# Opening of a decoder trunk: the first tiles of x on two DMA queues, the positions behind them

## The chip, the cores and the metric

The kernel runs on one core of a Trainium2 chip. The metric is the device time of one execution in microseconds (us). Five engines of the core work side by side, each through its own instructions in order: TensorE (PE in the rows, its weight loads PEld), VectorE (DVE), ScalarE (ACT), GpSimd (POOL) and SyncE (SP), which only issues DMAs here. A DMA that SP or ACT issues is put into that engine's queue; all queues share 16 DMA engines. An instruction that waits holds up everything behind it on its engine.

## The reference, cut to what matters

Two layers of a conditioned decoder trunk on x, 512 tokens of width 1024, in float32. Each layer normalises x, modulates it by a vector made from the condition c, and multiplies by a wide weight matrix. Cut to what the opening of the kernel computes:

```python
cos, sin = rope_tables(positions, x.dtype)
c_act = jax.nn.silu(c)
ada = jnp.einsum('bd,de->be', c_act, w_ada[l]) + b_ada[l]
sh_m, sc_m, g_m, sh_f, sc_f, g_f = jnp.split(ada, N_ADA, axis=-1)
h = modulate(rmsnorm(x, norm_mix_g[l]), sh_m, sc_m)
proj = jnp.einsum('bsd,de->bse', h, w_in[l])
# ... convolutions, differential attention, gates, MLP, a second layer, final norm
```

## The kernel before, in words

Activations lie transposed on the chip: 128 features on the partitions, 512 tokens along the row. So x, which comes in eight tiles `xin[2 * i + hh]` of 128 tokens and 512 features (256 KB each, tile family `cv`), is turned on TensorE by 128x128 transposes into eight tiles `xT[0]` to `xT[7]`. The four tiles of hh = 0 hold what `xT[0]` to `xT[3]` need, the four of hh = 1 the rest. Each turn (`x_turned`) is four transposes into one of three PSUM buffers of the family `t`, and one copy out of it by ACT (a unit `x`) or by DVE (a unit `v`).

The order of the opening is written out by hand in the string `START`. A unit is a letter and a number: `x`, `v` turn x; `y` squares a tile of x on ACT for the norm; `i` steps the task that loads and turns the parameter rows (`prm`); `a` steps `angles`, the rotary angles on DVE from the positions; `e`, `d` are the parts of the first modulation vectors that DVE sums up (into `part`), `r`, `s` the parts that TensorE sums up from `w_ada`; `c`, `t`, `q` bring these to columns (`ada`, `gsc`); `n`, `b` make the norm's factor and spread it; `m` makes a pair of h tiles from xT; `h`, `l` split a quarter of a weight tile into a rounded part and its remainder; `p` is a share of the first four products. Each engine sees its own instructions of these units in this order.

`w_ada` and the first weights of `w_in` come in four quarters, each of eight and two DMAs of 256 KB, all on SP behind x (families `qk`, `o`, `v`, `raw`). The DMAs of SP and ACT take turns on eight semaphores; an issue waits until the DMA that had its semaphore before has landed, so up to eight are under way. In the opening before, SP issues the positions (256 KB, the same 2 KB row to 128 partitions), then the eight tiles of x; ACT issues c and the small table `rc`; POOL the parameter rows. After the opening a planner keeps TensorE fed, and nothing there has a fixed time.

The second pair of h tiles (unit `m1`) stands on DVE behind unit `e2`, which reads the last `o` tile of the third quarter; TensorE's product `p6` reads that pair.

Of the kernel before, what the change touches and what calls it, by code (L numbers as in the profile page):

```python
# [17 lines left out]
P = 128  # L18
D = 1024
S = 512  # L20
# [14 lines left out]

ON_DVE = ((2, 3), (1, 5), (8, 3), (3, 7))
START = (
# [39 lines left out]
def kernel(  # L77
# [7 lines left out]
    nc = tc.nc  # L85
    V, A, T, G = nc.vector, nc.scalar, nc.tensor, nc.gpsimd
# [19 lines left out]
    def slot(tag, dt=F32, shape=None):  # L106
        return slots.tile(shape or [P, S], dt, tag=tag, name=nm(tag), bufs=SLOTS[tag])
# [79 lines left out]
    def params(l, eng=None):  # L187

        prm[l] = const.tile([P, NROW], F32, name=f"prm{l}")
        groups = (  # L190
            (
                (C_BADA, 48, b_ada[l].rearrange("(a p) -> a p", p=P)),
                (C_NMIX, 8, norm_mix_g[l].rearrange("(a p) -> a p", p=P)),
            ),
            (
                (C_NMLP, 8, norm_mlp_g[l].rearrange("(a p) -> a p", p=P)),
                (C_CAB, 4, conv_a_b[l].rearrange("(a p) -> a p", p=P)),
                (C_LNG, 4, ln_a_g[l].rearrange("(a p) -> a p", p=P)),
                (C_LNB, 4, ln_a_b[l].rearrange("(a p) -> a p", p=P)),
                (C_CBW, 12, conv_b_w[l].rearrange("k (a p) -> (k a) p", p=P)),  # L200
                (C_SUB, 1, subln_g[l].rearrange("(a p) -> a p", p=P)),
                (C_FG, 8, final_g.rearrange("(a p) -> a p", p=P)),
            ),
        )
        for gi, grp in enumerate(groups):
            c0, n = grp[0][0], sum(g[1] for g in grp)
            prow = ftile(F32, [n, P])
            for r0, m_, src in grp:
                G.dma_start(prow[r0 - c0 : r0 - c0 + m_, :], src)
            yield 15  # L210
            pt = ps_t()
            T.transpose(pt[:, :n], prow, ident[:n, :n])
            yield 1
            V.tensor_copy(prm[l][:, c0 : c0 + n], pt[:, :n])
            written.add((l, gi))
            yield 1
        V.tensor_scalar(out=subg[:, l : l + 1], in0=prm[l][:, C_SUB : C_SUB + 1],
                        scalar1=1.0 - lam_init[l], scalar2=None, op0=ALU.mult)
        written.add((l, "sub"))
# [900 lines left out]
    crow = ftile(F32, [8, P])  # L1120
    A.dma_start(crow, c.rearrange("b (a p) -> (b a) p", p=P))
    rc = const.tile([P, 2], F32, name="rc")
    A.dma_start(rc, rope_c)
    posi = slot("at", I32)
    nc.sync.dma_start(posi, positions.to_broadcast([P, S]))
    prm_task = params(0)
    next(prm_task)
    x2 = x.rearrange("b s d -> (b s) d")
    xin = [None] * 8
    for hh in range(2):  # L1130
        for i in range(NTB):
            t = xin[2 * i + hh] = slot("cv")
            nc.sync.dma_start(t, x2[i * P : (i + 1) * P, hh * 512 : (hh + 1) * 512])
    stage = iter(["qk"] * 16 + ["o"] * 8 + ["v"] * 8)

    def fetch(v, qt):
# [85 lines left out]
    def turn(row):  # L1222

        pt = ps_t()
        for a in range(4):
            T.transpose(pt[:, a * P : a * P + P], row[:, a * P : a * P + P], ident)
        return pt
# [92 lines left out]
    def rows_copy(qt):  # L1320
# [8 lines left out]
        i=lambda _: next(prm_task),  # L1329
        z=lambda _: next(lam_task),  # L1330
# [8 lines left out]
        t=lambda qt: q_cols.update({qt: turn(q_rows[qt])}),  # L1339
# [61 lines left out]
```

## Time and profile before

| what | value |
|---|---|
| time, median of 3 runs | 1890.07 us (1889.49 to 1890.42) |
| the profiled execution's own time | 1890.15 us |
| its span, first to last instruction | 1888.4 us |
| PE busy | 1868.8 us, 99% of the span |
| DVE, ACT, POOL busy | 66%, 42%, 3% |
| chain that ended last, by engine | PE 96%, DMA 2%, DVE 1% |

The span is followed from its first instruction; the profiled execution is 1.75 us longer than it. The chain of work that ended last is followed back from the last instruction, at each step to what released it. Idle time of an engine is printed with what ended it. A PE row that reads busy may still hold short waits, since ends of matmuls are modelled.

### The profile page before, as it was taken

How to read it: one execution, taken by the hardware profiler on the slowest of the kernel's cores; microseconds unless marked ns; L12 is line 12 of the kernel's file. 1: busy time of each engine (PE TensorE's matmuls, PEld its weight loads, DVE VectorE, ACT ScalarE, POOL GpSimd, SP SyncE). 2: the span in 40 equal slices, each digit the busy share in tenths (PEclk: the TensorE clock that was granted, in tenths of full speed). 3: DMA queues.
4: the chain of work that ended last, by engine and by line, in shares of the span. 5: the costliest groups of instructions: out<-in, count | busy, mean ns of one | idle time of the engine just before them, and what ended most of it. 6: DMA issues, size and time to landing. Idle time of an engine off the chain costs nothing.

```text
span 1888.4 us, 24857 instructions
## 1 busy us (share of the span) xinstructions
PE 1868.8 (99%) x9565; PEld 1597.4 (85%) x9565; DVE 1254.1 (66%) x2139; ACT 788.5 (42%) x1428; POOL 62.8 (3%) x109
## 2 busy tenths in 40 slices
PE   8999999999999999999999999999999999999998
PEld 6888888888889888888898888888888898888888
DVE  7788678997776656565677887798764563333336
ACT  4666652222433524233445665322243353424253
POOL 2001010000000000000000000000000000000000
PEclk9999999999999999999999999999999999999999
DMA  8644323444454455555535442222223422232221
GB/s 274 180 131 125 94 90 106 128 135 158 149 195 128 150 183 182 178 187 186 168 99 145 127 123 90 82 97 89 90 79 100 142 82 89 90 105 96 90 90 68
DMA packets 211142, 240.67 MB, mean 127 GB/s; under 512 B 10280, under 2 KB 178352, under 8 KB 211024
## 3 DMA queue, kind: packets, MB, share of 16 engines
q1 hardware_dynamic: 210096, 238.85, 40.5%
q8 instruction: 75, 1.23, 0.3%
q0 software_dynamic: 768, 0.23, 0.1%
q14 instruction: 43, 0.35, 0.1%
q10 hardware_dynamic: 160, 0.01, 0.0%
HBM read 216.50 MB, written 2.10 MB: 116 GB/s over the span
## 4 chain that ended last, share of the span: by engine, by line
PE 96%; DMA 2%; DVE 1%; issue 0%; SPq 0%; ACT 0%; POOLq 0%; POOL 0%; DVEq 0%; ACTq 0%
PE mm L150 86%; PE s L150 3%; PE t L827 2%; PE s L798 1%; PE s L797 1%; PE t L815 1%; DMA qk<-in_w_ada_dram 1%; PE t L460 0%; PE t L308 0%; PE t L835 0%; DMA f<-f 0%; DMA o<-in_w_ada_dram 0%; DMA cv<-in_x_dram 0%; DMA raw<-in_w_in_dram 0%; PE t L452 0%
## 5 line engine op out<-in xcount | busy, mean ns | idle before, releaser
L150 PE MATMUL mm<-h,wh 128*128 128x512 f32 x2720 | 850.7, 392 | 0.0
L150 PEld LDWEIGHTS mm<-h,wh 128*128 128x128 f32 x2720 | 508.0, 188 | 102.5 <-issue 0.7
L150 PE MATMUL mm<-h,wl 128*128 128x512 f32 x1360 | 532.1, 391 | 0.0
L399 ACT CAST wh<-raw 128x1024 fp32r<-128x1024 f32 (+1 forms) x308 | 308.7, 1005 | 404.2 <-PE mm L150 354.7
L407 DVE TENSOR_TENSOR wl<-raw,wh 128x1024 fp32r<-128x1024 f32 (+1 forms) x308 | 357.9, 1166 | 78.5 <-ACT wh L399 75.6
L150 PE MATMUL mm<-qk,wh 128*128 128x512 f32 (+1 forms) x1024 | 300.5, 376 | 0.0
L150 PEld LDWEIGHTS mm<-h,wl 128*128 128x128 f32 x1360 | 255.5, 188 | 52.1 <-issue 0.2
L150 PEld LDWEIGHTS mm<-qk,wh 128*128 128x128 f32 x1024 | 188.2, 188 | 35.1
L150 PE MATMUL mm<-qk,wl 128*128 128x512 f32 (+1 forms) x512 | 192.6, 376 | 0.0
L935 DVE SCALAR_TENSOR_TENSOR cv<-v,caw,cv 128x511 f32<-128x511 f32 (+14 forms) x240 | 175.9, 733 | 4.0
L504 DVE SCALAR_TENSOR_TENSOR xT<-mm,ada,xT 128x512 f32<-128x512 f32 (+1 forms) x81 | 56.0, 691 | 151.6 <-PE mm L150 151.5
L286 DVE SCALAR_TENSOR_TENSOR araw<-araw,cact,araw 128x512 f32<-128x512 f32 x140 | 104.6, 747 | 23.1 <-DMA araw<-in_w_ada_dram 22.7
L150 PEld LDWEIGHTS mm<-qk,wl 128*128 128x128 f32 x512 | 96.4, 188 | 17.2
L1082 ACT ACTIVATE f<-mm 128x512 f32<-128x512 f32 x60 | 35.9, 598 | 160.6 <-PE mm L150 157.1
L150 PE MATMUL mm<-o,wh 128*128 128x512 f32 (+1 forms) x320 | 95.2, 380 | 0.0
L150 PE MATMUL mm<-v,wh 128*128 128x512 f32 (+1 forms) x320 | 94.9, 379 | 0.0
L150 PE MATMUL mm<-wh,h 128*128 128x256 f32 x448 | 85.1, 284 | 0.0
L768 ACT ACTIVATE cv<-cv,st 128x128 f32<-128x128 f32 (+3 forms) x128 | 70.9, 556 | 18.3 <-DVE st L761 17.9
L1049 ACT ACTIVATE f<-mm 128x512 f32<-128x512 f32 x38 | 22.7, 598 | 132.4 <-PE mm L150 132.3
L443 POOL TENSOR_TENSOR st<-st,nhalf 128x4 f32<-128x4 f32 (+2 forms) x29 | 32.2, 1111 | 1360.9 <-DVE st L465 1007.5
L1056 DVE SCALAR_TENSOR_TENSOR f<-f,mm 128x512 f32<-128x512 f32 x38 | 26.1, 687 | 76.2 <-PE mm L150 76.1
L474 DVE TENSOR_TENSOR qk<-f,qk 128x512 fp32r<-128x512 f32 x38 | 26.3, 691 | 74.3 <-ACT qk L471 74.2
(263 smaller groups left out, 2324.8 us busy)
## 6 DMA issues: line engine op xcount, KB each, us to landing
raw<-in_w_in_dram SPq DMA_DIRECT2D x66, 1024.0 KB, 5.2
raw<-in_w_ff_dram SPq DMA_DIRECT2D x64, 1024.0 KB, 5.3
araw<-in_w_ada_dram SPq DMA_DIRECT2D x160, 256.0 KB, 2.9
raw<-in_w_c_out_dram SPq DMA_DIRECT2D x8, 1024.0 KB, 5.0
raw<-in_w_out_dram SPq DMA_DIRECT2D x8, 1024.0 KB, 5.1
f<-f SPq DMA_DIRECT2D x120, 64.0 KB, 2.1
qk<-qk SPq DMA_DIRECT2D x48, 128.0 KB, 2.3
qk<-in_w_ada_dram SPq DMA_DIRECT2D x16, 256.0 KB, 6.0
```

What stands on the lines that cost most here:

```text
L150: T.matmul(ps, lhsT, rhs, start=start, stop=stop)
L286: V.scalar_tensor_tensor(out=part, in0=r, scalar=cact[:, k : k + 1], in1=part, op0=ALU.mult, op1=ALU.add)
L399: A.copy(h_, r_)
L407: V.tensor_tensor(l_, r_, h_.bitcast(F32), op=ALU.subtract)
L443: G.tensor_tensor(y, v[:, :n], nhalf[:, :n], op=ALU.pow)
L474: V.tensor_tensor(lo, src, hi.bitcast(F32), op=ALU.subtract)
L504: V.scalar_tensor_tensor(out=xT[e][:, t0:t1], in0=pp[:, t0:t1], scalar=g[:, e : e + 1], in1=xT[e][:, t0:t1], op0=ALU.mult, op1=ALU.add)
L768: A.activation(p[cc][:, :n], p[cc][:, :n], AF.Exp, bias=nb[:, cc : cc + 1], scale=-1.0, accum_out=l0[:, i : i + 1] if cc == 0 else s1)
L827: T.matmul(po[:, j * P :], v[j // 2][x_][:, c0 : c0 + P], tiles[j][y_], start=j == 0 and i == 0, stop=j == NTB - 1 and i == 2)
L935: V.scalar_tensor_tensor(out=ac[:, s:], in0=glu[j][:, : S - s], scalar=wk, in1=ac[:, s:], op0=ALU.mult, op1=ALU.add)
L1056: V.scalar_tensor_tensor(out=t, in0=t, scalar=1.0, in1=pp, op0=ALU.add, op1=ALU.mult)
L1082: A.activation(r, pp, AF.Relu)
```

## The change

The order of first DMAs, the order of the units in the first sixth of `START`, and nothing else. The positions go from SP's first place to the end of ACT's issues, `rc` with them. Of the four tiles of hh = 0, two go to SP and two to ACT; SP's other DMAs follow as before. In `START` the turning of x (`x1`, `v0`, `x2`, `v3`) now precedes the parameter rows (`i0`), the squares take the tiles in the order of issue, and the last turn of the first half (`v3`) no longer stands behind `e0`.

```diff
 START = (
-    "i0 a0 y1 x1 a1 a2 y0 i1 y2 a3 v0 a4 x2 v7 y3 a5 v5 e0 y4 y7 y6 y5 v3 n h2 d0 r0 h0 l2 z "
+    "y0 x1 a0 y2 v0 a1 a2 y4 x2 y6 a3 v3 i0 y1 a4 v7 i1 y3 a5 v5 e0 y5 y7 n h2 d0 r0 h0 l2 z "
...
     A.dma_start(crow, c.rearrange("b (a p) -> (b a) p", p=P))
     rc = const.tile([P, 2], F32, name="rc")
-    A.dma_start(rc, rope_c)
     posi = slot("at", I32)
-    nc.sync.dma_start(posi, positions.to_broadcast([P, S]))
     prm_task = params(0)
     next(prm_task)
...
             t = xin[2 * i + hh] = slot("cv")
-            nc.sync.dma_start(t, x2[i * P : (i + 1) * P, hh * 512 : (hh + 1) * 512])
+            (A if hh == 0 and i > 1 else nc.sync).dma_start(
+                t, x2[i * P : (i + 1) * P, hh * 512 : (hh + 1) * 512])
+    A.dma_start(rc, rope_c)
+    A.dma_start(posi, positions.to_broadcast([P, S]))
```

Line numbers of the changed kernel are one higher from here on (the angles' first line is L1171 before, L1172 now).

On DVE, at the start of the program, these are the rows before, from the angles' cast of the positions (`at<-at`, an `a` unit) to the first `part`. `COPY xT` is a turned tile of x leaving PSUM, `COPY prm` the parameter rows.

```order
L1171 CAST at_222<-at_120 128x512
L1172 TENSOR_SCALAR at_222<-at_222,rc 128x512
L1174 TENSOR_SCALAR at_223<-at_222 128x512
L1176 TENSOR_SCALAR at_223<-at_223 128x512
L1179 SCALAR_TENSOR_TENSOR at_222<-at_223,at_222 128x512
L214 COPY prm_122<-t_253 128x56
L1179 SCALAR_TENSOR_TENSOR at_222<-at_223,at_222 128x512
L1242 COPY xT_104<-t_274 128x512
```

And now the same place, to the copy of the parameter rows:

```order
L1172 CAST at_222<-at_119 128x512
L1173 TENSOR_SCALAR at_222<-at_222,rc 128x512
L1243 COPY xT_104<-t_265 128x512
L1175 TENSOR_SCALAR at_223<-at_222 128x512
L1177 TENSOR_SCALAR at_223<-at_223 128x512
L1180 SCALAR_TENSOR_TENSOR at_222<-at_223,at_222 128x512 x2
L1243 COPY xT_107<-t_285 128x512
L1180 SCALAR_TENSOR_TENSOR at_222<-at_223,at_222 128x512
L1243 COPY xT_111<-t_296 128x512
L214 COPY prm_120<-t_291 128x56
```

The cast that waits for the positions is still DVE's first work on arrived data; two more copies of xT, and the copy of the parameter rows, now stand behind it.

On PE, before, the parameter rows (`t_253`) came first and the six turns followed (the first two rows of each turn shown here for the first and the last):

```order
L1155 MATMUL t_216<-ident,f_116 128x8
L212 MATMUL t_253<-ident,f_123 128x56
L1237 MATMUL t_259<-ident,cv_126 128x128
L1237 MATMUL t_259<-ident,cv_128 128x128
...
L1237 MATMUL t_313<-ident,cv_130 128x128
L1237 MATMUL t_313<-ident,cv_132 128x128
L1216 MATMUL t_330<-qk_144,cact 128x256 x2
```

Now four turns come first, then the parameter rows (`t_291`), two turns, and the first product with `w_ada` (`t_330`):

```order
L1238 MATMUL t_285<-ident,cv_128 128x128
L1238 MATMUL t_285<-ident,cv_130 128x128
L212 MATMUL t_291<-ident,f_121 128x56
L1238 MATMUL t_296<-ident,cv_132 128x128
...
L1238 MATMUL t_307<-ident,cv_136 128x128
L1238 MATMUL t_307<-ident,cv_138 128x128
L1217 MATMUL t_330<-qk_144,cact 128x256 x2
```

The three PSUM buffers of family `t` go round in the order of these names. So `t_330` takes the buffer that `t_291` had, `t_291` that of `t_265`, `t_307` that of `t_285`; each waits for the copy out of its predecessor, all three of them copies of DVE. Before, `t_330` took the buffer of `t_287`.

On ACT, the issues now stand ahead of the table load:

```order
L1121 DMA f_116<-in_c_dram 8x128
L1131 DMA cv_128<-in_x_dram 128x512
L1131 DMA cv_130<-in_x_dram 128x512
L1133 DMA rc<-rope_c_dram 128x2
L1134 DMA at_119<-in_positions_dram 128x512
L1158 ACT_TABLE_LOAD
```

Before, only c and rc stood there. SP keeps six of the eight tiles of x as its first DMAs, in place of the positions and eight.

## Rows read from the trace of the kernel before

**Rows 1.** Chain that ended last, first 40 us: start us, us, what.

```profile
2.58 6.19 DMA cv<-in_x_dram
...
26.41 7.12 DMA o<-in_w_ada_dram
...
36.90 2.80 PE s L150 x11
```

**Rows 2.** Busy time by stretch: stretch, length, engines' busy us, PEclk, DMA share, GB/s.

```profile
2.00:6.00 4.00, 0.24 (x1) 0.18 (x1) 0.72 (x3) 1.21 (x2) 1.24 (x2) 1.00 0.73 185
6.00:8.00 2.00, 0.00 (x0) 0.00 (x0) 1.38 (x4) 0.00 (x0) 0.00 (x0) 1.00 1.06 401
16.00:33.00 17.00, 16.86 (x86) 14.16 (x86) 14.93 (x40) 8.80 (x17) 4.28 (x7) 1.00 1.10 348
40.00:42.00 2.00, 2.00 (x11) 1.65 (x10) 1.86 (x5) 0.21 (x1) 0.00 (x0) 1.00 0.24 79
```

**Rows 3.** Timeline of PE, 8 to 37 us: start, us, operation [idle before <-releaser].

```profile
8.72 0.32 PE L212 MATMUL t<-ident,f 56*128 56x56 f32 x1 [6.22 <-DMA f<-in_norm_mix_g_dram]
8.98 4.84 PE L1237 MATMUL t<-ident,cv 128*128 128x128 f32 x24
13.66 2.75 PE L1216 MATMUL t<-qk,cact 128*128 128x256 f32 x12
...
16.68 2.32 PE L1216 MATMUL t<-qk,cact 128*128 128x256 f32 x10
18.84 0.59 PE L1219 MATMUL t<-part,ones 128*128 128x256 f32 x2
19.27 0.60 PE L1237 MATMUL t<-ident,cv 128*128 128x128 f32 x4
19.71 0.60 PE L460 MATMUL t<-ident,st 128*128 128x128 f32 x4
```

**Rows 4.** The same at 35 to 37 us, where PE reaches p6.

```profile
35.31 0.59 PE L1219 MATMUL t<-part,ones 128*128 128x256 f32 x2
36.11 0.49 PE L150 MATMUL s<-h,wh 128*128 128x512 f32 x1 [0.21 <-ACT h L492]
```

**Rows 5.** Timeline of DVE around e2, 32 to 35 us.

```profile
32.81 0.36 DVE L1206 TENSOR_SCALAR part<-o,cact 128x256 f32<-128x256 f32 x1 [0.86 <-DMA o<-in_w_ada_dram]
33.63 1.01 DVE L1209 SCALAR_TENSOR_TENSOR part<-o,cact,part 128x256 f32<-128x256 f32 x2 [0.46 <-DMA o<-in_w_ada_dram]
```

**Rows 6.** Timeline of DVE, 5 to 19 us.

```profile
5.61 0.43 DVE L1171 CAST at<-at 128x512 f32<-128x512 int32 x1 [1.99 <-DMA at<-in_positions_dram]
6.58 0.49 DVE L1172 TENSOR_SCALAR at<-at,rc 128x512 f32<-128x512 f32 x1 [0.54 <-DMA rc<-rope_c_dram]
7.10 0.43 DVE L1174 TENSOR_SCALAR at<-at 128x512 f32<-128x512 f32 x1
...
8.03 0.69 DVE L1179 SCALAR_TENSOR_TENSOR at<-at,at 128x512 f32<-128x512 f32 x1
9.09 0.22 DVE L214 COPY prm<-t 128x56 f32<-128x56 f32 x1 [0.37 <-PE t L212]
...
13.84 0.69 DVE L1183 SCALAR_TENSOR_TENSOR at<-at,at 128x512 f32<-128x512 f32 x1
14.44 0.68 DVE L1242 COPY xT<-t 128x512 f32<-128x512 f32 x1
15.04 0.34 DVE L1206 TENSOR_SCALAR part<-qk,cact 128x256 f32<-128x256 f32 x1
...
17.44 1.00 DVE L1209 SCALAR_TENSOR_TENSOR part<-qk,cact,part 128x256 f32<-128x256 f32 x2 [0.20 <-DMA qk<-in_w_ada_dram]
```

**Rows 7.** Timeline of ACT, first 10 us.

```profile
1.75 1.28 ACT L1157 ACT_TABLE_LOAD   x1 [1.75 <-issue]
...
9.28 0.63 ACT L1248 ACTIVATE f<-cv 128x512 f32<-128x512 f32 x1 [6.06 <-DMA cv<-in_x_dram]
```

**Rows 8.** SP's timeline, one issue.

```profile
9.95 0.37 SPq L1141 DMA_DIRECT2D qk<-in_w_ada_dram  x1
```

**Rows 9.** Waits of SP's queue, first 12 us: us in total, times, longest.

```profile
SPq L1133 <- DMA at<-in_positions_dram: 1.4, 1, 1.4
```

## The prediction, made before the run

> **What bounds the kernel now.** I read three views: the chain of work that ended last, the busy time by stretch, and the timelines of PE and DVE through the first 40 us. The chain is TensorE for 96% of the span, and all that the change touches lies in its first 40 us, where it is something else: from 2.58 us to 33.53 us it is DMA after DMA, each issued when an earlier one had landed, from a tile of x at 2.58 to the `o` tile issued at 26.41 [rows 1]. From 36.90 on it is TensorE. The stretches say why: 401 GB/s from 6 to 8 us, 348 GB/s from 16 to 33 us with the DMA engines full, and the stream is over at about 40 us, when 79 GB/s are left in the stretch from 40 to 42 [rows 2]. So the opening is a full stream of about 12 MB, and TensorE and DVE keep pace behind it.
>
> The place where stream and engines meet is the product `p6`. DVE waits 0.86 and 0.46 us for the last two `o` tiles [rows 5], then makes the h tiles that `p6` reads. TensorE ends its work ahead of it at 35.74 (two instructions of 0.216 us from 35.31; the length from ten in 2.16 us), does one matmul, and runs without a break only from 36.90 [rows 1, 3, 4]. With 0.23 us for that one matmul, TensorE has 36.90 - 35.74 - 0.23 = 0.93 us to spare there, and DVE 1.32 us. Any delay of the opening up to 0.93 us vanishes at `p6`, and nothing that only makes TensorE earlier moves it. Behind `p6` TensorE has no DMA of fixed time to wait for, so what is late or early there stays so to the end.
>
> **The stream.** The bytes and their order by size stay: positions, x, four quarters. The one part that isn't full is the ramp: 185 GB/s from 2 to 6 us. Against 401 GB/s that is 4 x 216 = 864 KB short, or 2.2 us [rows 2]. If two queues or another first transfer healed all of it, the last `o` tile would land 2.2 us earlier; that is one end. The other end is 0: before, SP already had six tiles of x under way before it had to wait for the positions (1.4 us in all [rows 9]), so the DMA engines were not short of work, and the row of positions must still be moved, only later. I take 0, because the stream had queued work throughout the ramp.
>
> The Trainium skill, page "DMA: Bandwidth & Descriptors", section "Issuing engines are not separate DMA queues", says that issuing from several engines saves issue time on the sequencer and nothing else, since all of it runs on the same DMA engines. By that rule the gain of the stream is 0, by the ramp's full repair it is 2.2 us. No run so far shows which.
>
> **The issues.** SP loses three issues; its `w_ada` issues wait for landings anyhow, so this is worth nothing. ACT gains three issues, some 0.4 us each, ahead of its table load at 1.75 us [rows 7]. These 1.2 us lie under ACT's idle 6.06 us before its first square at 9.28 [rows 7]. The tanh behind the table load feeds `cact`, which DVE first needs for `part` at 15.04 and TensorE at 13.66 [rows 3, 6]. Cost 0; without that cover it would be 1.2 us.
>
> **The positions, on DVE.** This is the term that decides. The rotary cast stays DVE's first work on arrived data, and it waits for the positions. Before, they landed at 5.6 us as the first transfer [rows 6]. Now they are behind two tiles of x on ACT's queue while SP's holds four. Whether the DMA engines serve the two queues in turn or by time of issue, about six tiles of x go ahead of them. The rows give the time at which so many transfers had landed before: the fifth at 8.78 (the chain's tile of x, 2.58 + 6.19), the sixth at 9.28 (ACT's first square), the seventh at 9.95 (SP's issue that waited for it) [rows 1, 7, 8]. So P, the landing of the positions, goes from 5.6 to between 8.8 and 9.95; if the ramp is healed by the full 2.2 us, to 6.6 at the lowest. I take 9.4, near the sixth row.
>
> Behind the cast on DVE now stand the copies of `xT[0]`, `xT[3]`, `xT[7]` and then that of the parameter rows. TensorE's first `w_ada` product takes the PSUM buffer of those rows, so it waits for that copy. From P: 0.43 + 0.49 for the cast and the product with rc; 0.60 for `xT[0]`; 0.93 for two operations (7.10 to 8.03); 0.69 for the angle step that needs its result at once; 0.60 each for another angle step, `xT[3]`, a third angle step and `xT[7]` (the distance of 13.84, 14.44 and 15.04); 0.22 for the parameter rows [rows 6]. The sum is 5.8 us. So the `w_ada` product starts at P + 5.8, against 13.66 before, where it waited only for TensorE itself. Then 12 instructions of 0.216 us, 2 of them, and 10 more, 5.2 us in all, to the last L1219, which stood at 18.84 [rows 3]. Now it stands at P + 11.0. DVE's own way to that point (a last angle step, `xT[5]`, `e0`, the norm's three small steps, `d0`, some 4.3 us behind the parameter rows) ends at P + 10.1 and hides under it.
>
> The two are equal at P = 7.85. With P = 9.4 the last L1219 comes at 20.4, 1.55 us late. From there to `p6` TensorE and DVE run nearly without idle time, so the delay is carried on; 0.93 us of it vanish at `p6`, and 0.6 us remain. That the turning of x now starts before the parameter rows (TensorE waited 6.22 us for them [rows 3]) gains nothing: the turned tiles wait in PSUM for DVE, which waits for the positions. `v3` taken from behind `e0` gives DVE 0.60 us there, in a place that no longer ends last.
>
> **Sum.** 1890.15 + 0.6 = 1890.8 us against the profiled execution; that lies 0.08 above the median, so 1890.7 us is the forecast. Its own bounds: P = 8.8 gives 0, P = 9.95 gives +1.2 us, so 1890.1 to 1891.3.
>
> **The rivals.** (1) The stream ends earlier. For it: the ramp's 2.2 us, and the positions' one row read 128 times may be what was slow. Against it: the row is still read. It needs the positions early too, as `p6` moves by the stream's gain only if P is at most 8.8 less that gain. With half the ramp, 1.1 us, P must be 7.7, and the time is 1889.0; with all of it 1887.9.
>
> (2) Slower by TensorE's pace. The first 24 transposes took 4.7 us from 8.98 to 13.66, and four later ones take 0.44 us from 19.27 to 19.71 [rows 3]: at that pace 24 would take 2.6. The granted clock reads 1.00 in the stretches shown [rows 2], so I cannot say from it whether those 2.1 us are waits or pace. If they are pace that sets in only after TensorE has worked for a while, the change hurts: the turns come early, TensorE then idles until DVE has copied, twice, and pays the slow start again in the `w_ada` product. That adds up to the same 2.1 us to the last L1219; with P = 9.4 it is 3.65 us late, less 0.93, so 1892.8 us; with P = 9.95, 1893.4. It decides from the point where TensorE stands idle ahead of `t_330` for as long as its work before was short. The Trainium skill, page "TensorE: Matmul & The Clock Gate", Part 1, states such a rule: the array starts at 1.2 GHz and goes to 2.4 GHz under sustained work. The 1.00 of the granted clock doesn't bear it out here, the spacing of the transposes does.
>
> (3) It doesn't do what it says: the four tiles land no earlier than before, as they share the DMA engines with all else. Then P is at its late end, 9.95, and the time 1891.2 us; it is the upper half of the forecast.
>
> **How the numbers follow.** Forecast with (3): 0.52, 1890.1 to 1891.3. Rival (2): 0.26, 1891.3 to 1893.4. Rival (1): 0.17, 1887.9 to 1890.1. The rest, 0.05, is a further wait that I don't see, on the slow side. Leaving out a tenth at each end gives 1888.6 to 1893.3. The bound of 0.2%, about what a measurement of this kernel can tell from no change, is 3.8 us: faster needs 1886.3, below all of the ramp; slower needs 1893.9, above rival (2). So faster 0.02, within 0.93, slower 0.05.
>
> **What would show it.** DVE's cast of the positions at about 9.4 us (before 5.61) and TensorE's first `w_ada` product at about 15.2 us make the main step right; a cast before 7.9 makes it wrong. The wait of DVE for the last `o` tile at 33.6 shrinking to nothing, and `p6` at about 37.5, show the loss; `p6` before 36 would show rival (1). `w_ada` instructions more than 0.216 us apart, with their tiles landed, would show rival (2). A difference behind 40 us that isn't there at `p6` would make the whole argument wrong.

## The result, and the profile after

The changed kernel takes 1893.23 us (median; 1891.15 to 1894.15), the kernel before 1889.80 us (1888.83 to 1890.54) beside it: a ratio of 1.0018, interval 1.0012 to 1.0023, so 2.3 to 4.3 us longer. The ratio lies within the 0.2% that were called no change, its interval reaches just beyond, and the time lies 0.07 us under the upper end of the range (1893.3), not in the forecast's own bounds. The profiled execution took 1892.8 us with a span of 1891.0, 2.65 us more than the one before.

TensorE's timeline after, where before it had [rows 3] (start, us, operation, idle before and what ended it):

```profile
4.01 0.48 PE L1238 MATMUL t<-ident,cv 128*128 128x128 f32 x1 [1.41 <-DMA cv<-in_x_dram]
...
8.15 3.03 PE L1238 MATMUL t<-ident,cv 128*128 128x128 f32 x13 [1.98 <-DMA cv<-in_x_dram]
11.43 0.27 PE L212 MATMUL t<-ident,f 56*128 56x56 f32 x1 [0.25 <-DVE xT L1243]
11.62 0.66 PE L1238 MATMUL t<-ident,cv 128*128 128x128 f32 x4
14.28 0.99 PE L1238 MATMUL t<-ident,cv 128*128 128x128 f32 x4 [2.00 <-DVE xT L1243]
15.48 4.02 PE L1217 MATMUL t<-qk,cact 128*128 128x256 f32 x12 [0.21 <-DVE xT L1243]
19.33 0.60 PE L1220 MATMUL t<-part,ones 128*128 128x256 f32 x2
19.76 2.32 PE L1217 MATMUL t<-qk,cact 128*128 128x256 f32 x10
21.92 0.59 PE L1220 MATMUL t<-part,ones 128*128 128x256 f32 x2
```

The first tiles of x are turned from 4.01 us on, as the change wants it, but the first `w_ada` product (15.48) is 1.82 us later than before (13.66), and the last L1220 (21.92) 3.08 us. The other 1.26 us are in the first twelve instructions: from 15.48 to 19.33 they take 3.85 us, before 16.25 - 13.66 = 2.59. The row of the kernel before that ends them:

```profile
16.25 0.59 PE L1219 MATMUL t<-part,ones 128*128 128x256 f32 x2
```

DVE's timeline after, the same time (it answers to [rows 6]), to the copy of the parameter rows:

```profile
9.82 0.43 DVE L1172 CAST at<-at 128x512 f32<-128x512 int32 x1 [4.56 <-DMA at<-in_positions_dram]
...
14.73 0.69 DVE L1243 COPY xT<-t 128x512 f32<-128x512 f32 x1
15.34 0.21 DVE L214 COPY prm<-t 128x56 f32<-128x56 f32 x1
```

DVE stands idle for 4.56 us until the positions land at 9.80, then works without a break to the copy of `xT[7]` at 14.73, which the trace names as what the product waited for. The prediction had named the copy behind it, that of the parameter rows; but this one ends at 15.55, after the product's start at 15.48, so it is not what released it, though by the order of the buffers it should be. The two are 0.1 us apart. The chain that ended last has the same: its first 15 us were DMA after DMA before [rows 1], and are now the positions and DVE.

```profile
2.73 7.07 DMA at<-in_positions_dram
...
9.82 0.44 DVE at L1172
...
14.82 0.61 DVE xT L1243
...
15.48 4.02 PE t L1217 x12
```

The stretches of after (columns as in [rows 2]):

```profile
2.00:6.00 4.00, 1.50 (x4) 0.72 (x4) 0.33 (x2) 2.07 (x4) 1.24 (x2) 1.00 0.83 259
6.00:8.00 2.00, 0.17 (x1) 0.00 (x0) 0.00 (x0) 0.00 (x0) 0.00 (x0) 1.00 0.98 307
...
14.00:20.00 6.00, 5.51 (x20) 4.41 (x21) 5.79 (x16) 1.14 (x4) 1.45 (x2) 0.72 1.10 349
16.00:33.00 17.00, 16.87 (x80) 14.19 (x79) 14.30 (x36) 7.96 (x16) 3.30 (x5) 0.95 1.10 347
```

The ramp carries more at first (259 GB/s from 2 to 6 us, before 185) and less right behind (307 from 6 to 8 us, before 401), and then the stream runs as before (347, before 348). From 14 to 20 us the granted clock is 0.72: part of that stretch ran at 1.2 GHz, right behind TensorE's 2.00 us of idle time. SP's issue that waits for the first `w_ada` tile tells that the stream's start gained nothing: 12.06 us after, 12.09 before. The last `o` tile lands about 1 us earlier than before (issued at 26.5 and some 6 us under way, against 33.53), but DVE reads it only at 35.33, so nothing hangs on it.

```profile
12.06 1.13 SPq L1152 DMA_DIRECT2D raw<-in_w_in_dram  x2
```

```profile
12.09 1.11 SPq L1151 DMA_DIRECT2D raw<-in_w_in_dram  x2
```

At `p6` I compare the third matmul of it, the first that reads `wl`. Before (first fence) it starts at 37.23, after (second fence) at 39.27, 2.04 us later. TensorE no longer waits there, and DVE no longer waits for `o` tiles as in [rows 5].

```profile
37.23 0.40 PE L150 MATMUL s<-h,wl 128*128 128x512 f32 x1
```

```profile
38.62 0.82 PE L150 MATMUL s<-h,wh 128*128 128x512 f32 x2
39.27 0.39 PE L150 MATMUL s<-h,wl 128*128 128x512 f32 x1
```

So 3.08 us at the last L1220 are 2.04 at `p6`: 1.04 us were absorbed.

### The profile page after: what moved, and what is told of

Read it like the earlier page. It is cut to its first block, busy times and chain, and to the rows that moved or that the text cites. A ratio compares the mean times of both kernels' runs of the same rounds, so it can differ in the third digit from the quotient of the medians.

```text
span 1891.0 us, 24858 instructions
## 1 busy us (share of the span) xinstructions
PE 1870.8 (99%) x9565; PEld 1599.0 (85%) x9565; DVE 1253.7 (66%) x2139; ACT 787.6 (42%) x1428; POOL 62.7 (3%) x109
## 4 chain that ended last, share of the span: by engine, by line
PE 96%; DVE 1%; DMA 1%; ACT 1%; issue 0%; SPq 0%; ACTq 0%; POOLq 0%; POOL 0%; DVEq 0%
PE mm L150 85%; PE s L150 3%; PE t L827 2%; PE s L798 1%; PE t L815 1%; PE s L797 1%; PE t L1217 1%; PE t L460 0%; DMA f<-f 0%; PE t L308 0%; PE t L835 0%; DMA at<-in_positions_dram 0%; DMA raw<-in_w_in_dram 0%; SPq L722 0%; DVE wl L407 0%
```

## The experiments

The theory after the result: two causes, the start of the first `w_ada` product, which DVE sets, and TensorE's pace in its first twelve instructions. Rivals: the split over two queues, the new order of units by itself, or the stream. All medians below stand against the kernel before, run on the same chip beside them (1889.7 to 1890.1 us); intervals are about 1.7 us to either side, so the traces tell more than the times of single kernels. Each trace is of one execution, though, and lies up to 1.4 us from the median of its kernel (e1 1.4 above, e3 0.9 and e2 0.7 above; f3 and f1 1.0, e5 0.8 and e6 0.7 below). The table gives what each trace shows: first product, its first twelve instructions, the last L1219 or L1220, and how much later than before the third matmul of `p6` starts. Products "without readers" are the unit `w`: 128x128 products of the identity by itself, of two instructions each.

| kernel | DMA order | first product | twelve | last L1219/20 | at p6 | median |
|---|---|---|---|---|---|---|
| before | before | 13.66 | 2.59 | 18.84 | 0 | 0 |
| after | after | 15.48 | 3.85 | 21.92 | +2.04 | +3.4 |
| after, another execution (f4) | after | 15.97 | 3.66 | 22.22 | +2.30 | |
| START of before (e1) | after | 15.76 | 3.49 | 21.84 | +1.97 | +1.6 |
| START of after (e2) | before | 14.92 | 4.29 | 21.80 | +1.92 | +1.5 |
| positions first (e4) | split, positions first | 15.53 | 3.80 | 21.92 | +2.04 | +2.7 |
| products added late (e3) | after | 16.20 | 2.59 | 21.38 | +1.51 | +3.0 |
| products added early and late (e5) | after | 15.40 | 2.69 | 20.68 | +0.80 | +2.4 |
| the same, START of after (e6) | before | 14.58 | 2.59 | 19.76 | -0.04 | +0.7 |
| angle steps spread (e7) | after | 13.74 | 3.87 | 20.20 | +1.22 | +1.8 |
| angle steps spread, products (f2) | after | 14.46 | 2.59 | 19.98 | +0.31 | +1.1 |
| before, products (f1) | before | 12.83 | 2.59 | 18.61 | -0.22 | +0.7 |
| before, other source (e8) | before | 13.47 | 2.60 | 18.66 | -0.81 | -0.5 |
| positions as one row (f3) | one row | 14.71 | 2.59 | 19.89 | +0.01 | +1.9 |

One rule gives the column "at p6" from the two before it: the last L1219 or L1220 less 18.84 less 1.04 us (the figure from after, so that only the other rows test it), or the landing of the last `o` tile against before (33.53), whichever is later. For e1 that is 1.96, e2 1.92, e3 1.50, e4 2.04, e5 0.80, f3 0.01 by TensorE; for e6 -0.04, f1 -0.23, f2 +0.31 and e8 -0.81 by the `o` tile, which landed at 33.49, 33.30, 33.84 and 32.72. Only e7 is off, by 0.90, for which see there.

**Each half of the change alone** (e1_old_start, e2_new_start). The first has the changed DMAs and this edit to START, the second the old DMAs and its reverse:

```diff
-    "y0 x1 a0 y2 v0 a1 a2 y4 x2 y6 a3 v3 i0 y1 a4 v7 i1 y3 a5 v5 e0 y5 y7 n h2 d0 r0 h0 l2 z "
+    "i0 a0 y1 x1 a1 a2 y0 i1 y2 a3 v0 a4 x2 v7 y3 a5 v5 e0 y4 y7 y6 y5 v3 n h2 d0 r0 h0 l2 z "
```

> The DMA order of the changed kernel with the START of the kernel before. Theory (positions late, and DVE's stream held behind their cast): the cast still stands at 9.8 us, as the positions still come last; DVE needs about 5.3 us from there to the copy whose PSUM buffer the first w_ada product takes, so that product starts at about 15.1 us (before 13.66, changed kernel 15.48), the last L1219/L1220 at 20.3 us at full TensorE pace or 21.5 us at the pace of the changed kernel; behind p6 0.5 to 1.7 us remain, 1890.4 to 1891.6 us. Rival (the new order of units, not the late positions, costs the time): the time of the kernel before, 1889.8 us or less.

> The DMA order of the kernel before with the START of the changed kernel. Theory (positions late): the cast is back at 5.6 us, the first w_ada product starts as soon as TensorE has turned x, not later than 14 us, the last L1219 at 19.0 us or earlier, p6 is again set by the stream: 1889.8 us, plus or minus 0.4. Rival (the new order of units costs the time by itself): 1892 us or more, and the first w_ada product behind 15 us.

Measured: 1891.38 us, 1.0007 (0.9998 to 1.0016), and 1891.29 us, 1.0006 (0.9997 to 1.0015). For e1 the theory holds: the cast is at 10.03 and the product late. It comes at 15.76 and not at the 15.1 expected, because TensorE's last twelve transposes, the first of which waits for DVE's copy of the parameter rows (12.54), run at the slow pace up to it:

```profile
12.80 3.17 PE L1238 MATMUL t<-ident,cv 128*128 128x128 f32 x12 [0.53 <-DVE prm L214]
```

For e2 the theory fell: the cast is early, and the time is still lost. DVE's timeline of e2 shows why:

```profile
5.43 0.43 DVE L1171 CAST at<-at 128x512 f32<-128x512 int32 x1 [1.82 <-DMA at<-in_positions_dram]
6.61 0.49 DVE L1172 TENSOR_SCALAR at<-at,rc 128x512 f32<-128x512 f32 x1 [0.74 <-DMA rc<-rope_c_dram]
10.12 0.69 DVE L1242 COPY xT<-t 128x512 f32<-128x512 f32 x1 [3.03 <-PE t L1237]
...
14.78 0.20 DVE L214 COPY prm<-t 128x56 f32<-128x56 f32 x1
```

In the new START the copy of `xT[0]` stands ahead of the angle steps, so DVE waits 3.03 us for x to be turned, with angle instructions behind it that could have run; before, three of them ran from 7.10 to 8.72 [rows 6]. Either half alone makes the first product late, in e2 through DVE's copies, which end at 14.98 there and at 15.55 with both. TensorE's twelve instructions are the slowest of all here, 4.29 us. In the traces the two losses overlap: 1.97 and 1.92 us at `p6`, and 2.04 together. The medians don't bear that out: 1.6 and 1.5 us, and 3.4 together. e1's trace is of the longest of its eleven executions (1892.82 us), and e2's eleven fall into two groups, five from 1889.72 to 1890.40 us and six from 1891.29 to 1892.35, with its trace in the second. So it isn't shown that the losses overlap in the usual execution as well.

**The split with the positions first** (e4_posi_first), the changed kernel with one DMA put back:

```diff
+    nc.sync.dma_start(posi, positions.to_broadcast([P, S]))
...
-    A.dma_start(posi, positions.to_broadcast([P, S]))
```

> The changed kernel with one edit: the positions are SP's first DMA again, so that the first four tiles of x are still split over two queues but stand behind the positions; rc stays behind the tiles on ACT. Theory (the late positions are the whole loss): the cast stands at 5.6 to 6 us, the first w_ada product not later than 14 us, no loss at p6: 1889.8 us, plus or minus 0.4. Rival (the split over two queues costs time by itself, by issues on ACT or by transfers that get in each other's way): 1891 us or more with the cast at 6 us.

Measured: 1892.48 us, 1.0014 (1.0005 to 1.0022). Not the expected 1889.8: the cast came at 5.79, but `rc`, now behind the tiles of x on ACT's queue, held DVE's second instruction until 10.04 (3.83 us), in the place of the positions, and START is the new one. It doesn't separate the split's own price. What the traces say of that: SP's issue behind the first `w_ada` tile stands at 11.92 to 12.52 us in the eight with the split, and at 12.00 to 12.20 in the four without it that read the row 128 times (before, e2, e6, f1). The split widens the spread; a price or a gain of it doesn't show.

```profile
5.79 0.43 DVE L1172 CAST at<-at 128x512 f32<-128x512 int32 x1 [1.20 <-DMA at<-in_positions_dram]
10.04 0.49 DVE L1173 TENSOR_SCALAR at<-at,rc 128x512 f32<-128x512 f32 x1 [3.83 <-DMA rc<-rope_c_dram]
```

**TensorE's pace** (e3_warm, e5_after_warm, e6_new_start_warm). The edits to the changed START, that of e3 first; e5 has the second, and e6 has it with the old DMAs:

```diff
-    "y0 x1 a0 y2 v0 a1 a2 y4 x2 y6 a3 v3 i0 y1 a4 v7 i1 y3 a5 v5 e0 y5 y7 n h2 d0 r0 h0 l2 z "
+    "y0 x1 a0 y2 v0 a1 a2 y4 x2 y6 a3 v3 i0 y1 a4 v7 i1 y3 a5 w9 v5 w2 e0 y5 y7 n h2 d0 r0 h0 l2 z "
```

```diff
-    "y0 x1 a0 y2 v0 a1 a2 y4 x2 y6 a3 v3 i0 y1 a4 v7 i1 y3 a5 v5 e0 y5 y7 n h2 d0 r0 h0 l2 z "
+    "w12 y0 x1 a0 y2 v0 a1 a2 y4 x2 y6 a3 v3 i0 y1 a4 v7 i1 y3 a5 w9 v5 w1 e0 y5 y7 n h2 d0 r0 h0 l2 z "
```

> The changed kernel with eleven more 128x128 products on TensorE, whose results nobody reads, put where TensorE stands idle ahead of the last turns and of the first w_ada product. Theory (1.26 us of the loss is TensorE's pace after its idle time): the granted clock of 14 to 20 us reads 1.00 in place of 0.72, the first twelve w_ada instructions take 2.6 us in place of 3.85, and the time falls by about 1.2 us, to 1892.0 us. Rival (the pace of those twelve is something else, such as tiles that land late, or the lost time is regained later anyway): they take 3.8 us again, or the time stays at 1893.2 us.

> The changed kernel with 22 products more on TensorE whose results nobody reads: twelve ahead of the first turn, where TensorE waits for x, nine ahead of the last turn of the first six and one behind it (each is two instructions). Theory (of the 3.1 us that the last L1220 is late, 1.8 are the late start of the first w_ada product and 1.3 are TensorE's pace, and the two add): the start stays at 15.5 us, since DVE sets it; the first twelve instructions take 2.6 us; the last L1220 starts at 20.7 us, 0.9 us more are left at p6 than before, so about 1892.0 us, 1.2 below the changed kernel. Rival (pace counts for nothing, as the order of DVE's work alone sets the end): the last L1220 and the time as in the changed kernel, 1893.2 us.

> The DMA order of the kernel before, the START of the changed kernel, and the same 22 products without readers as in the run with the DMA order of the changed kernel. Theory (the start order loses its time twice, by DVE's angle steps that now stand behind the first copy of xT, and by TensorE's pace after idle time): TensorE turns at 0.1 us apiece, the copy of xT and all behind it on DVE start about 0.5 us earlier, the first w_ada product at 14.4 us, the last L1219 at 19.6 us, 0.7 us late, which TensorE's spare 0.9 us at p6 hide: 1889.8 us, in place of 1891.3. Rival (the pace is not the cause): 1891.3 us again.

Measured: e3 1892.80 us, 1.0016 (1.0007 to 1.0025), 0.8 above the expected time; e5 1892.18 us, 1.0012 (1.0003 to 1.0021), as expected; e6 1890.48 us, 1.0005 (0.9996 to 1.0014), 0.7 above. In e3 the twelve instructions have the full pace (2.59 us), but at TensorE's pace ahead of them nine products were too many and moved the first product to 16.20; of 1.26 us only 0.54 were gained at the last L1220. The granted clock of 1.00 that was expected there is no evidence, since f4 reads 1.00 in the same stretch at the slow pace (below). In e5 the twelve more ahead of the first turn cured that:

```profile
2.42 5.04 PE L1255 MATMUL s<-ident 128*128 128x128 f32 x24
7.30 0.49 PE L1238 MATMUL t<-ident,cv 128*128 128x128 f32 x3
8.22 1.66 PE L1238 MATMUL t<-ident,cv 128*128 128x128 f32 x13 [0.43 <-DMA cv<-in_x_dram]
...
15.40 2.86 PE L1217 MATMUL t<-qk,cact 128*128 128x256 f32 x12 [0.32 <-DVE xT L1243]
18.09 0.59 PE L1220 MATMUL t<-part,ones 128*128 128x256 f32 x2
...
20.68 0.59 PE L1220 MATMUL t<-part,ones 128*128 128x256 f32 x2
```

Thirteen transposes take 1.66 us in place of 3.03, and the last L1220 starts at 20.68, as expected to 0.02 us. The start is DVE's, the pace is TensorE's, and at the last L1220 they add: 1.74 + 0.10 us here, 1.82 + 1.26 in the changed kernel. In e6 nothing is left at `p6`. That the pace of the twelve hangs on what TensorE did ahead of them is shown: 2.59 to 2.69 us in the six kernels with added products, 3.49 to 4.29 in after, f4, e1, e2, e4 and e7. Whether the pace was lost by idle time or not yet reached differs; f4 below shows both. The medians bear it out in direction only, as e5 against after is 1.0 us in the medians and 1.24 at `p6`.

**The angle steps behind the copies** (e7_angles_spread, f2_spread_warm), both with the changed DMAs, positions last; e7 first, then f2:

```diff
-    "y0 x1 a0 y2 v0 a1 a2 y4 x2 y6 a3 v3 i0 y1 a4 v7 i1 y3 a5 v5 e0 y5 y7 n h2 d0 r0 h0 l2 z "
-    "h3 a6 l0 s0 c0 h1 l3 l1 x6 b t0 q0 m0 e1 d1 h4 x4 h7 l4 h6 e2 r1 l6 p2 p3 s1 a7 c1 p0 t1 "
+    "y0 x1 y2 v0 a0 y4 x2 y6 v3 i0 y1 i1 v7 y3 v5 a1 a2 e0 a3 y5 y7 n h2 d0 r0 h0 l2 a4 z "
+    "h3 a5 l0 s0 c0 h1 l3 a6 l1 x6 b t0 q0 m0 e1 d1 h4 x4 h7 l4 h6 e2 r1 l6 p2 p3 s1 a7 c1 p0 t1 "
```

```diff
-    "y0 x1 a0 y2 v0 a1 a2 y4 x2 y6 a3 v3 i0 y1 a4 v7 i1 y3 a5 v5 e0 y5 y7 n h2 d0 r0 h0 l2 z "
+    "w12 y0 x1 y2 v0 a0 y4 x2 y6 v3 i0 y1 i1 v7 y3 v5 w9 a1 a2 e0 a3 a4 y5 y7 n h2 a5 d0 r0 h0 l2 z "
```

> The DMA order of the changed kernel, with the positions last, but in START the angle steps spread: the cast behind the first copy of xT by DVE, the next two behind all copies, the others behind e0 and d0; the copy of the parameter rows ahead of the copy of xT[7]. Theory (it isn't the late landing itself, but that DVE's copies stand behind the cast that waits for it): the first copy of xT stands at 9.5 us, ahead of the cast, the first w_ada product starts at 13.3 us, the last L1220 not later than 19 us, no loss at p6: 1889.3 us, plus or minus 0.5 (the last o tile, which landed at 32.4 to 33.5 us in the runs so far, sets p6 again). Rival (the late positions cost DVE its capacity wherever the steps stand): DVE is behind at d0 and the last L1220 at 20 us or later, 1891 us or more.

> The DMA order of the changed kernel with both repairs: the angle steps spread behind DVE's copies of xT, and 21 products without readers, twelve ahead of the first turn and nine ahead of the first w_ada product. Theory (order on DVE and TensorE's pace are the whole loss, the late positions as such cost nothing): the first w_ada product at about 13.7 us, its twelve instructions in 2.6 us, the last L1220 at 19.3 us or earlier, and p6 is set by the last o tile again: 1889.3 us, plus or minus 0.5. Rival (the late positions take DVE time that it lacks later): the last L1220 early, but DVE late at m1 with no wait for the last o tile, and 1890.5 us or more.

Measured: 1891.55 us, 1.0010 (1.0001 to 1.0019), and 1891.19 us, 1.0006 (0.9997 to 1.0015). In e7 the first product is at 13.74 as hoped with the positions still last, so DVE's order was the cause of the late start, not the landing as such. But the twelve instructions took 3.87 us, so that the last L1220 (20.20) and the time are those that the rival had named; 1.28 us of it is pace, not DVE. And TensorE waited 0.69 us more at 23.60, in a place where DVE has the steps that were moved. The traces tell what that wait hangs on: in before, after, e6, f2 and e7 alike this product starts 0.26 to 0.32 us behind the start of DVE's second `ada<-t` (23.34 in e7), and in e7 three angle steps (19.61 to 21.48) stand ahead of it that are done earlier in the others. That is read from the traces and not tested by an edit. In f2 both repairs are in, and `p6` is 0.31 us late because the last `o` tile landed 0.31 us later. DVE waits for it again:

```profile
33.95 1.00 DVE L1210 SCALAR_TENSOR_TENSOR part<-o,cact,part 128x256 f32<-128x256 f32 x2 [0.26 <-DMA o<-in_w_ada_dram]
```

So the expected mechanism is there, but the median is 1.9 us above the 1889.3 expected; part of it arises behind `p6` (below). By the time alone the rival (1890.5 or more) is nearer, but its sign, no wait for the last `o` tile, isn't there.

**The stream and the one row** (e8_distinct, f3_row_on_chip), both on the kernel before, e8 first:

```diff
-    nc.sync.dma_start(posi, positions.to_broadcast([P, S]))
+    nc.sync.dma_start(posi, x.rearrange("b s d -> (b s) d")[:P, :S].bitcast(I32))
```

```diff
-    "i0 a0 y1 x1 a1 a2 y0 i1 y2 a3 v0 a4 x2 v7 y3 a5 v5 e0 y4 y7 y6 y5 v3 n h2 d0 r0 h0 l2 z "
+    "a0 w12 i0 y1 x1 a1 a2 y0 i1 y2 a3 v0 a4 x2 v7 y3 a5 v5 w5 e0 y4 y7 y6 y5 v3 n h2 d0 r0 h0 l2 z "
...
-    nc.sync.dma_start(posi, positions.to_broadcast([P, S]))
+    A.dma_start(posi[:1, :], positions)
...
-        V.tensor_copy(ang, posi)
-        V.tensor_scalar(out=ang, in0=ang, scalar1=rc[:, 0:1], scalar2=None, op0=ALU.mult)
+        V.tensor_copy(ang[:1, :], posi[:1, :])
+        pp = ps_s()
+        T.matmul(pp, ones1[:1, :].to_broadcast([1, P]), ang[:1, :], start=True, stop=True)
+        V.tensor_scalar(out=ang, in0=pp, scalar1=rc[:, 0:1], scalar2=None, op0=ALU.mult)
```

> The kernel before, with another source for the DMA of the positions: 256 KB of x in 128 rows of their own in place of one 2 KB row read 128 times, so that the angles are computed from other numbers; the work is the same. Theory (the stream's start doesn't depend on that row): the first w_ada tile lands at 12.05 us as in the runs so far, and the time is 1889.8 us. Rival (the one row read 128 times makes the ramp slow): the 256 KB land well before 5.4 us, the first w_ada tile up to 2.2 us earlier, and as TensorE has 0.9 us to spare at p6, the time is about 1888.9 us.

> The kernel before with the positions read once, as one row of 2 KB to one partition, and spread over the partitions by one product on TensorE; twelve products without readers behind it and five ahead of the last turn of the six keep TensorE's pace. Theory (the 256 KB of positions are bytes in a full stream, and the row read 128 times is slow besides): the first w_ada tile lands at about 11.0 us in place of 12.07, the last o tile about 1 us earlier than with the same place of the long fetch, p6 as much earlier since TensorE has 0.9 us to spare: 1888.9 us, plus or minus 0.4, below both kernels. Rival (TensorE or DVE take over as the bound at p6): 1889.8 us.

Measured: 1889.22 us, 0.9998 (0.9989 to 1.0007), and 1892.04 us, 1.0011 (1.0002 to 1.0020). In e8 the 256 KB from 128 rows (those of the first tile of x, which the next DMA reads again) are there for the cast at 3.67 us, in place of 5.61, and SP's issue behind the first `w_ada` tile stands at 11.68:

```profile
3.67 0.43 DVE L1171 CAST at<-at 128x512 f32<-128x512 int32 x1
```

```profile
11.68 1.13 SPq L1151 DMA_DIRECT2D raw<-in_w_in_dram  x2
```

So the row read 128 times does cost its own DMA some 1.9 us, but the stream only 0.4 at its start and 0.8 at the last `o` tile, not 2.2. The time moved by no more than can be measured. In f3 the row is read once, the first tile of x landed at 3.56, and the first `w_ada` tile in the trace at 11.31; but the products that I had put ahead of the parameter rows ran until 10.59, and that work took over:

```profile
6.27 4.39 PE L1256 MATMUL s<-ident 128*128 128x128 f32 x24
10.59 0.27 PE L212 MATMUL t<-ident,f 56*128 56x56 f32 x1
```

That is the rival's case, with nothing gained at `p6`; the time is above what either had named. It says nothing against reading the row once; that was not tried without those products.

**TensorE early in the kernel before** (f1_before_warm), with this edit, and **the changed kernel once more** (f4_after_again), unaltered:

```diff
-    "i0 a0 y1 x1 a1 a2 y0 i1 y2 a3 v0 a4 x2 v7 y3 a5 v5 e0 y4 y7 y6 y5 v3 n h2 d0 r0 h0 l2 z "
+    "w12 i0 a0 y1 x1 a1 a2 y0 i1 y2 a3 v0 a4 x2 v7 y3 a5 v5 e0 y4 y7 y6 y5 v3 n h2 d0 r0 h0 l2 z "
```

> The kernel before with twelve products without readers (24 instructions) on TensorE ahead of its first turn, while it waits for the parameter rows and x. Theory (TensorE's slow first instructions are pace, and TensorE isn't what sets p6): the 24 transposes take about 0.11 us apiece in place of 0.2 where their buffers are free, the first w_ada product starts up to 1.5 us earlier, and the time stays at 1889.8 us, since p6 waits for the last o tile and DVE. Rival (TensorE's early work sets the end): 1889.0 us or less.

> The changed kernel once more, unaltered, for the trace of another execution. Theory (TensorE's pace in the opening comes and goes from execution to execution, at other places relative to the start): the cast at 9.8 us and the first w_ada product at 15.5 us again within 0.2 us, but the twelve instructions behind it take a time between 2.6 and 5.2 us that differs from the 3.85 of the first trace, and the span differs by about as much, less what p6 hides. Rival (the pace is fixed by the program): 3.85 us again, and the span within 0.3 us of 1891.0.

Measured: f1 1890.81 us, 1.0003 (0.9995 to 1.0012); f4's execution took 1892.66 us. In f1 the transposes run at twice the pace and the first product starts 0.83 us earlier, at 12.83; DVE's wait for the last `o` tile is there again, and `p6` moves by that tile's 0.23 us alone:

```profile
8.74 1.53 PE L1237 MATMUL t<-ident,cv 128*128 128x128 f32 x12
```

```profile
33.40 1.00 DVE L1209 SCALAR_TENSOR_TENSOR part<-o,cact,part 128x256 f32<-128x256 f32 x2 [0.36 <-DMA o<-in_w_ada_dram]
```

So a faster TensorE gains nothing there. In f4 the twelve took much the same time (3.66 us against 3.85), so the expected swing was not seen there. It is seen ahead of them: the four transposes that take 0.66 us in after (11.62) take 1.11 in f4 (first fence). So in after TensorE had the full pace by then and lost it right behind the 2.00 us of idle time that follow; in f4 it had not reached it yet. The column of the granted clock shows the fall in after (0.72 from 14 to 20 us) and reads 1.00 in f4 (second fence). e2 goes with after (0.72, and 0.66 us for the four), e4, e7 and e1 with f4 (1.00, and 1.11 us for four, 1.97 for eight, 3.17 for twelve transposes).

```profile
12.21 1.11 PE L1238 MATMUL t<-ident,cv 128*128 128x128 f32 x4
...
15.97 3.82 PE L1217 MATMUL t<-qk,cact 128*128 128x256 f32 x12
```

```profile
14.00:20.00 6.00, 5.14 (x18) 4.14 (x19) 5.79 (x16) 1.68 (x5) 0.96 (x1) 1.00 1.07 352
```

The cast came later in f4, at 10.32, and all behind it:

```profile
10.32 0.43 DVE L1172 CAST at<-at 128x512 f32<-128x512 int32 x1 [5.17 <-DMA at<-in_positions_dram]
```

No kernel here beats the one before: the lowest median, e8's, computes from other numbers, and its interval holds 1.

## Why the prediction was right, and where it was wrong

The class was right: within 0.2%. The likeliest case was not: it said 1890.7 us with its own bounds to 1891.3, and rival (2), 1891.3 to 1893.4, is what came. That the time fell inside the stated range was partly luck. The range's ends don't follow from the chances: spread evenly within their intervals these give 1889.2 to 1893.0 us, which 1893.23 would have missed. And that rival (2)'s 1892.8 us is the traced execution's time is chance: it has 2.7 us at `p6` and nothing behind it, the trace 2.04 and 0.61. By the steps:

- **The stream, taken as 0**: right. The issue behind the first `w_ada` tile stands at the same time, 12.06 against 12.09. The Trainium skill, page "DMA: Bandwidth & Descriptors", section "Issuing engines are not separate DMA queues", says that a second issuing engine saves issue time alone; this row agrees. The bound of 2.2 us was far too wide, since e8, which takes away the slow transfer itself, brings 0.4 at the first `w_ada` tile and 0.8 at the last `o` tile.
- **The issues on ACT, taken as 0**: right. `cact` comes at 5.10 in place of 3.46, and its first reader on TensorE is at 15.48.
- **The landing P, taken as 9.4, bounds 8.8 to 9.95**: 9.80, and 10.30 in f4, which is above the bound; 0.4 us of the miss.
- **DVE from P to the first product, 5.8 us**: 15.48 - 9.80 = 5.68, and 15.97 - 10.30 = 5.67 in f4. Right in size, and the step that was named as the main one. The copy that it ends with is not: the trace has the product released by the copy of `xT[7]`, so the 0.22 us of the parameter rows in the sum are not part of the wait, and the rest took 0.1 longer.
- **TensorE from there to the last L1220, 5.2 us**: this step failed. It is 6.44 us. I had taken the pace of [rows 3] from where the kernel before had long been busy, so the forecast's sum put the slow pace at nothing; it was 1.26 us, where rival (2) had up to 2.1. The chance of 0.26 for that rival was too low: the spacing of the 24 transposes had shown the slow pace already, and the order showed TensorE idle ahead of the product. The Trainium skill, page "TensorE: Matmul & The Clock Gate", Part 1, says that the array starts at 1.2 GHz, and the spacing agrees: 13 transposes take 1.66 us in e5 behind added products, 3.03 in after.
- **0.93 us absorbed at p6**: 1.04, right to a tenth, and it held in seven of the eight other traces in which TensorE sets `p6`.
- **Behind p6 nothing has a fixed time**: wrong in part. 2.04 us at `p6` became 2.65 at the end; by the prediction's own last sign such a difference speaks against its argument. TensorE waits for DVE in a few places there, and DVE for the DMAs `f<-f` of the rotary step, whose wait at the second place below is 1.34 us before, 1.09 after and 0.63 in e4. TensorE after, at the two places (first fence), before at the second place (second fence), and e4 there (third):

```profile
105.59 0.44 PE L815 MATMUL t<-ident,cv 128*128 128x128 f32 x2 [0.64 <-DVE caw L229]
...
1028.92 0.77 PE L815 MATMUL t<-ident,cv 128*128 128x128 f32 x5 [1.41 <-DVE cv L777]
```

```profile
1026.28 0.76 PE L815 MATMUL t<-ident,cv 128*128 128x128 f32 x5 [1.19 <-DVE cv L777]
```

```profile
1024.47 0.69 DVE L724 TENSOR_TENSOR f<-f,sin_t 128x512 f32<-128x512 f32 x1 [0.63 <-DMA f<-f]
...
1027.71 0.76 PE L815 MATMUL t<-ident,cv 128*128 128x128 f32 x5 [0.46 <-DVE cv L777]
```

In e4 the second place gives 0.7 us back; in after it takes 0.2, although DVE's wait for the DMA is shorter there, and the first takes 0.5 to 0.6. What sets these is not settled.

The terms then go: predicted 0.62; P and DVE's 5.68 us in place of 9.4 and 5.8, +0.28; the pace +1.26; 1.04 absorbed in place of 0.93, -0.11; together 2.05, and 2.04 was seen at `p6`; behind it +0.61, which makes 2.65. The medians lie 3.4 us apart, 0.8 more: that of after is 0.4 above its profiled execution, that of before 0.35 below its own, and neither is explained. Nor is it settled why the medians of the kernels with added products lie 0.7 to 1.9 us above what `p6` shows, and that of after 1.4. In the traces with added products TensorE stands idle 0.33 to 0.88 us between 79 and 82 us, again waiting for DVE behind a rotary DMA, as in f3:

```profile
80.23 0.50 PE L150 MATMUL mm<-h,wl 128*128 128x512 f32 x1 [0.88 <-DVE wl L407]
```

Why that DMA is later in them I did not find out.

## What to carry to other kernels

When a transfer is put at the back, look at the first instruction on each engine that waits for it and at all that stands behind that instruction; and look as well at where the copies that release PSUM now stand, since putting them first made DVE wait for TensorE, at the same price. In the traces here the two delays overlap, so that undoing one gains almost nothing at `p6`; in the medians undoing either gains 1.9 us, and which of the two holds for the usual execution is open. Work for TensorE that comes early but in pieces costs pace later: price the products behind an idle stretch at the slow spacing that the trace shows at the program's start.

## What the runs showed of the hardware

- The granted clock reads 1.00 from 8 to 14 us in the kernel before, where 24 transposes took 4.68 us (8.98 to 13.66 [rows 3]); in f1, with products ahead, twelve take about 1.5 us. In f4 it reads 1.00 from 14 to 20 us too, where twelve instructions took 3.66 us in place of 2.59. In the opening the spacing of like instructions tells the pace, and the column does not. The stretch of the kernel before:

```profile
8.00:14.00 6.00, 5.28 (x27) 4.95 (x28) 3.98 (x8) 4.59 (x13) 0.00 (x0) 1.00 1.08 363
```

- The same program was at the full pace at one point in one execution and not in another: four transposes took 0.66 us at 11.62 in after and 1.11 us at 12.21 in f4, and the twelve instructions behind the idle stretch were slow in both (3.85 and 3.66 us).
- One 2 KB row read to 128 partitions arrives some 1.9 us later than 128 different rows of the same size (4.9 and 2.9 us from issue to landing, cast at 5.61 and 3.67), while the stream behind it is put off by 0.4 us at its start.
- The last `o` tile, behind some 9 MB of a full stream, landed anywhere from 32.1 to 33.8 us in the executions that move all 256 KB of positions, whose first `w_ada` tile landed from 11.7 to 12.5 us: the bound that this stream sets has that much play.
